# The attention outputs of a first token block: seven heads loaded during the last head, the eighth after it; the norm vectors loaded on another queue

## The chip, the cores and the metric

The kernel runs on one core of a Trainium2 chip. The metric is the device time of one execution in microseconds (us), lower is better. Besides TensorE (PE, with PEld for its weight loads), the core has VectorE (DVE), ScalarE (ACT), GpSimd (POOL) and SyncE (SP); nearly all transfers are issued by SP.

## What is computed

A network of two layers on a sequence of 1024 tokens with width 1024, in float32. Only the first layer's token mixer and what follows it matter here:

```python
def block(args):                       # 8 heads, blocks of 128 queries
    logits = einsum(q_nope, k_nope) + einsum(q_rope, k_rope)
    logits = where(chunk_mask, logits * scale, NEG_BIG)
    p = softmax(logits)
    return einsum('bhqk,bkhd->bqhd', p, v)
o = from_blocks(map(block)).reshape(b, s, 8 * 128)
mix = o @ w_o
h = layernorm(ALPHA * h + mix, ln_mix_g, ln_mix_b)
h = layernorm(ALPHA * h + swiglu(h), ln_ffn_g, ln_ffn_b)
```

## The kernel before

**Products.** Each matrix product is made of three matmuls: every operand x is split into a high part (ACT casts it) and a low part (DVE or POOL subtracts the high part from x), and high·high, high·low and low·high are added up in PSUM (`mm3`, lines 168 to 170).

**First attention.** `attention` (line 278) goes over the heads; each has eight blocks of 128 queries. For a block, `score_a` makes the scores and the softmax, `turn_a` the transposed, split probabilities (the casts and subtractions of lines 264 and 265), and after every second block `mix_a` makes the product with the values for a group of 256 queries. Its result goes through a tile `ob` with two buffers (the reduction of line 1319 on DVE) and is stored to `o_dr[0][group][head]` in DRAM (line 1320). The last head takes its blocks in the order 6, 7, 4, 5, 2, 3, 0, 1, so that group 3 is stored first, group 0 last. `fill` holds other work that is called after a given block.

**Output projection.** `out_proj` (line 298) follows. It loads the two vectors of the layer norm on the GpSimd queue (line 177), loads and splits `w_o` head by head (lines 142, 146 and 147; the splits of heads 6 and 7 are held behind the attention's last casts), and takes the eight token blocks in the same order. For a block it loads the outputs of all eight heads, 128 partitions by 8 by 128 values, into a tile `of` (line 319), splits them in two halves of four heads each into `oh` and `ol` (lines 323 and 324), loads the residual rows into `z` (line 330), makes two halves of 512 columns with 24 matmuls each, adds them to `z` (line 338) and normalises (`layer_norm`). The first block's splits are held behind the attention's last cast and last subtraction:

```python
                    if prev is None:
                        behind(i.ins, newest["hi"])
                        behind(j.ins, newest["lo"])
```

`behind` keeps program order and waits for nothing. The program is written in a framework that makes the waits itself and that orders the instructions of each engine by priority (the order of the calls) and by its own estimate of when an instruction can start; an engine then takes them in that order. Memory is given out in pools, and a tile waits for the last readers of what lay in its place.

**After it.** `ffn` takes the normalised blocks, first transposed by `raw_x`.

Of the kernel before, what the change touches and what calls it, by code (L numbers as in the profile page):

```python
# [9 lines left out]
F32 = mybir.dt.float32  # L10
# [6 lines left out]
P = 128  # L17
S = 1024
D = 1024
NTB = S // P  # L20
KD = D // P
H = 8
# [16 lines left out]
LAST_ORDER = (6, 7, 4, 5, 2, 3, 0, 1)  # L39
# [3 lines left out]
def trunk(  # L43
# [32 lines left out]
    nc = tc.nc  # L76
# [9 lines left out]
    late = edge.tile([P, 504], F32, tag="edge", name="edge")  # L86
# [21 lines left out]
    def f32(t):  # L108
        return t.bitcast(F32)

    def big_tile(name, dt=F32R):
        return big.tile([P, 2, 1024], dt, tag="big", name=name)
# [20 lines left out]
    def small(name, n=1):  # L133
        return sp.tile([P, 2], F32, tag="small", name=name, bufs=22)[:, :n]
# [40 lines left out]
    def bcast_row(pool, src, n, name, tag, eng=None):  # L175
        t = pool.tile([P, n], F32, tag=tag, name=name, bufs=1)
        (eng or nc.gpsimd).dma_start(t, src.partition_broadcast(P))
        return t

    def behind(i, j):  # L180

        tc.add_manual_dep(
            i, j.name,
            mybir.DependencyInfo(mybir.DependencyClass.NoSync, mybir.DependencyReason.DATA),
            reason="kept in program order",
        )
# [91 lines left out]
    def attention(score, turn, mix, fill, la, hp):  # L278


        blocks = [(h, i) for h in range(H - 1) for i in range(NTB)] + [(H - 1, i) for i in LAST_ORDER]
        for fn in fill.get(-1, ()):
            fn()
        for b in range(la):
            score(*blocks[b])
        for b, (h, i) in enumerate(blocks):
            if b and i % 2 == 0:
                mix(blocks[b - 1][0], blocks[b - 1][1] // 2)
            if b + la < len(blocks):
                with tc.high_priority(hp[0]):  # L290
                    score(*blocks[b + la])
            with tc.high_priority(hp[1]):
                turn(h, i)
            for fn in fill.get(b, ()):
                fn()
        mix(blocks[-1][0], blocks[-1][1] // 2)

    def out_proj(side, w_o, o_dram, x_src, x_dst, lng, lnb, xo):


        with tc.tile_pool(name="op0", bufs=2, side=side, reuse_waits="tile") as pool:
            g = bcast_row(pool, lng, D, "mg0", "g")
            b = bcast_row(pool, lnb, D, "mb0", "b")
            wo = []
            for h in range(H):
                dst = ()
                if h in (0, 1, 2, 3, 7):
                    t = big_tile(f"wo0_{h}")
                    dst = (t[:, 0], t[:, 1])
                elif h == 6:  # L310
                    t = pool.tile([P, 2, D], F32R, tag=f"wo{h}", name=f"wo0_{h}", bufs=1)
                    dst = (t[:, 0], t[:, 1])
                wo.append(load_w(w_o[h], 1024, f"wo0_{h}", *dst, after=("hi", "scale") if h > 5 else ()))
            prev = None
            for tb in LAST_ORDER:
                nm = f"a0_{tb}"
                of = pool.tile([P, H, P], F32, tag="of", name=f"of_{nm}", bufs=2)
                src = o_dram[tb // 2][:, :, (tb % 2) * P:(tb % 2) * P + P]
                loaded = nc.sync.dma_start(of, src.rearrange("h p q -> p h q")).ins
                ot = pool.tile([P, 2, D], F32R, tag="oh", name=f"oh_{nm}").rearrange("p a (h q) -> p a h q", h=H)  # L320
                oh, ol = ot[:, 0], ot[:, 1]
                for hs in (slice(0, 4), slice(4, 8)):
                    i = A.copy(oh[:, hs], of[:, hs])
                    j = V.tensor_tensor(ol[:, hs], of[:, hs], f32(oh[:, hs]), ALU.subtract)
                    if prev is None:
                        behind(i.ins, newest["hi"])
                        behind(j.ins, newest["lo"])
                zy = pool.tile([P, 2, D], F32, tag="zy", name=f"zy_{nm}")
                z, y = zy[:, 0], zy[:, 1]
                behind(nc.sync.dma_start(z, x_src[tb * P:(tb + 1) * P, :]).ins, loaded)  # L330
                sums = small(f"sum_{nm}", 2)
                junk = []
                for nh in range(2):
                    c = slice(nh * 512, nh * 512 + 512)
                    m = (ps_m if nh == 0 else ps_t)(f"zp_{nm}_{nh}")
                    junk.append(m)
                    mm3(m, [(oh[:, h, :], ol[:, h, :], wo[h][0][:, c], wo[h][1][:, c]) for h in range(H)])
                    V.scalar_tensor_tensor(
                        z[:, c], z[:, c], ALPHA, m, ALU.mult, ALU.add, accum_out=sums[:, nh:nh + 1]
                    )  # L340
                if tb == LAST_ORDER[-1]:
                    y = big_tile(f"y_{nm}", F32)[:, 0]
                layer_norm(z, sums, junk, y, g, b, nm, x_dst[tb * P:(tb + 1) * P, :])
                if prev is not None:
                    raw_x(prev[1], xo, prev[0], f"a0_{prev[0]}")
                prev = (tb, y)
        return lambda: raw_x(prev[1], xo, prev[0], f"a0_{prev[0]}")
# [733 lines left out]
    o_dr = [[dr.tile([H, P, 256], F32, name=f"o_dr{l}_{g}") for g in range(4)] for l in range(2)]  # L1081
    zero_dr = dr.tile([P, 512], F32, name="zero_dr")
    wo_dr = [dr.tile([P, 2, D], F32, name=f"wo_dr{h}") for h in range(H)]
    xs_dr = [dr.tile([S, D], F32, name=f"xs_dr{l}") for l in range(3)]


    lat4 = [[big_tile(f"c{p}{hf}").rearrange("p a (b t) -> p (a b) t", b=2) for hf in range(2)] for p in range(2)]
    ast = ExitStack()
    krp = ast.enter_context(tc.tile_pool(name="krp", bufs=1))
    lat2 = [big_tile("ck_hi"), krp.tile([P, 2, S], F32R, tag="cklo", name="ck_lo")]  # L1090
# [9 lines left out]
    with tc.tile_pool(name="a0", bufs=2, side="right") as pool:  # L1100
# [53 lines left out]
            return ms  # L1154

        def latents(tb, hq, hk):
            junk = pool.tile([P, 384], F32, tag="junk", name=f"junk{tb}")
            ssq = small(f"ssq{tb}", 2)
            A.activation(junk, hq[:, :384], AF.Square, accum_out=ssq[:, 0:1])
            A.activation(junk[:, :256], hk[:, :256], AF.Square, accum_out=ssq[:, 1:2])  # L1160
            ve = small(f"cve{tb}", 2)
            V.tensor_scalar(ve[:, 0:1], ssq[:, 0:1], 1.0 / RQ, RMS_EPS, ALU.mult, ALU.add)
            V.tensor_scalar(ve[:, 1:2], ssq[:, 1:2], 1.0 / RKV, RMS_EPS, ALU.mult, ALU.add)
            rs = small(f"crs{tb}", 2)
            G.tensor_tensor(rs, ve, mhalf, ALU.pow)
            cn = pool.tile([P, 768], F32, tag="cn", name=f"cn{tb}")
            ra = pool.tile([P, 64], F32, tag="ra", name=f"ra{tb}")
            rb = pool.tile([P, 64], F32, tag="rb", name=f"rb{tb}")
            V.tensor_tensor(ra, hk[:, 256:320], kt[:, tb, 0:64], ALU.mult)
            V.tensor_tensor(rb[:, 0:32], hk[:, 288:320], kt[:, tb, 64:96], ALU.mult)  # L1170
            V.tensor_tensor(rb[:, 32:64], hk[:, 256:288], kt[:, tb, 96:128], ALU.mult)
            V.tensor_tensor(cn[:, 640:704], ra, rb, ALU.add)
            V.tensor_tensor(cn[:, 704:768], ra, rb, ALU.add)
            V.scalar_tensor_tensor(cn[:, :384], hq[:, :384], rs[:, 0:1], gq, ALU.mult, ALU.mult)
            V.scalar_tensor_tensor(cn[:, 384:640], hk[:, :256], rs[:, 1:2], gk, ALU.mult, ALU.mult)
            return cn
# [46 lines left out]
    with ast as st:  # L1223
        pool = st.enter_context(tc.tile_pool(name="a1", bufs=2, reuse_waits="tile"))
# [99 lines left out]
        def at(slot, fn, *args):  # L1324
            fill.setdefault(slot, []).append(lambda: fn(*args))
# [9 lines left out]
        for h in range(1, H):  # L1335
            b = 8 * (h - 1)
# [17 lines left out]
            nc.sync.dma_start(zero_dr, f32(t[:, :512]))  # L1354

        at(14, store_zeros)
        attention(score_a, turn_a, mix_a, fill, 2, (0, 0))

    banks("ps2", PS_BUFS)
# [14 lines left out]
        return new_xT(pool, "f0")  # L1374

    xo, stacks = x_pools("m0", "right")
    pending = out_proj("left", w_o_a, o_dr[0], x, xs_dr[0], ln_mix_g[0], ln_mix_b[0], xo)
    xT, rest, normed = ffn("left", xo, stacks, pending, 0, xs_dr[0], xs_dr[1], ln_ffn_g[0], ln_ffn_b[0], next_x)


    banks("ps3", PS_BUFS_B)
    with ExitStack() as st:
        lp = st.enter_context(tc.tile_pool(name="b1l", bufs=5, reuse_waits="tile"))
        pool = st.enter_context(tc.tile_pool(name="b1", bufs=2, reuse_waits="tile"))
# [9 lines left out]
        for ql in q_lo:  # L1394
            for mp in range(2):
                b = slice(64 - mp * 64, 128 - mp * 64)
# [135 lines left out]
        for h in range(1, H):  # L1532
            b = 8 * (h - 1)
# [13 lines left out]
        first, second = LAST_ORDER[:2]  # L1547
# [6 lines left out]
        b = 8 * (H - 1) - 2  # L1554
# [11 lines left out]
    xo, stacks = x_pools("m1", "left")  # L1566
    pending = proj[0].rest(ln_mix_g[1], ln_mix_b[1], xo)
# [91 lines left out]
```

## Time and profile before

| | |
|---|---|
| median of 3 runs | 2265.44 us (2265.01 to 2267.45) |
| profiled execution, span from first to last instruction | 2269.7 us |
| PE busy | 2238.7 us, 99% of the span |
| DVE, ACT, POOL busy | 1593.1, 1007.1, 886.3 us |
| data moved | 289.25 MB |

The profiled execution's own time is given by its span alone; it lies 4.3 us over the median of the timed runs. Matmuls are pipelined, so a busy PE need not be one at its peak. A row of a timeline gives the start, the duration, the engine, the line, the operation, the tiles, and in brackets how long the engine had been idle and which instruction ended that.

### The profile page before, as it was taken

To read this page: it belongs to the slowest core of one execution; us is meant where nothing else is said; L and a number is where in the kernel's file an instruction comes from. 1 tells how busy PE (TensorE), PEld (TensorE's weight loads), DVE (VectorE), ACT (ScalarE), POOL (GpSimd) and SP (SyncE) were. 2 spreads that over 40 slices of the span, in tenths; PEclk is the share of its full clock that TensorE was granted. 3 is DMA by queue.
4 is the path that set the end of the run, shared out by engine and by line. 5 is a ranking of instruction groups with operands and counts; after the bars stand their busy time and mean duration, and the time that the engine had idled before them with its cause. 6 is when DMAs were issued, how large, how long until landed. Compare 5 with 4: busy or idle time off the path is not lost.

```text
span 2269.7 us, 30075 instructions
## 1 busy us (share of the span) xinstructions
PE 2238.7 (99%) x10850; PEld 1883.5 (83%) x10850; DVE 1593.1 (70%) x2944; ACT 1007.1 (44%) x2077; POOL 886.3 (39%) x711
## 2 busy tenths in 40 slices
PE   9999999999999999999999999999999999999998
PEld 9888897878888888887888888877778888888886
DVE  6677774596656667778578777676586666568778
ACT  4455563352333334445466656555442332334444
POOL 2243451104544445555333435321014444446552
PEclk9999999999999999999999999999999999999999
DMA  6121335334324138454311212153334323247544
GB/s 207 41 95 59 121 98 186 116 145 148 139 70 139 70 114 335 177 199 153 112 43 33 61 35 64 42 209 114 137 132 150 108 83 126 82 150 269 204 171 159
DMA packets 104420, 289.25 MB, mean 127 GB/s; under 512 B 8656, under 2 KB 32080, under 8 KB 93776
## 3 DMA queue, kind: packets, MB, share of 16 engines
q1 hardware_dynamic: 100272, 277.90, 35.0%
q0 software_dynamic: 4000, 9.44, 1.5%
q8 instruction: 85, 1.39, 0.2%
q14 instruction: 63, 0.52, 0.1%
HBM read 205.78 MB, written 77.33 MB: 125 GB/s over the span
## 4 chain that ended last, share of the span: by engine, by line
PE 46%; DVE 5%; issue 1%; DMA 1%; ACT 1%; POOL 1%; POOLq 0%; DVEq 0%; SPq 0%; ACTq 0%
PE gb L565 8%; PE gc L565 5%; PE dw L871 4%; PE ga L565 4%; PE zp_a L440 3%; PE dx L871 3%; PE s_b L239 3%; PE bp L168 2%; PE bp L170 2%; PE bp L169 2%; PE bv L1409 2%; PE dv L871 1%; PE dy L871 1%; PE o_b L274 1%; PE pt_b L173 1%
## 5 line engine op out<-in xcount | busy, mean ns | idle before, releaser
L521 ACT CAST op_g<-gr 128x512 fp32r<-128x512 f32 x240 | 147.5, 622 | 403.5 <-PE gb L565 225.4
L521 POOL TENSOR_TENSOR op_g<-gr,op_g 128x512 fp32r<-128x512 f32 x104 | 146.1, 1410 | 303.4 <-DVE tmp L661 160.0
L521 DVE TENSOR_TENSOR op_h<-rh,op_h 128x512 fp32r<-128x512 f32 x154 | 164.0, 1090 | 58.8 <-ACT op_h L521 58.7
L565 PE MATMUL ga<-xh_m,op_g 128*128 128x512 f32 x512 | 168.0, 389 | 0.0
L871 PE MATMUL dw<-op_w_t,op_h 128*128 128x512 f32 x660 | 153.1, 391 | 1.8 <-DVE op_h L521 1.8
L521 ACT CAST op_h<-rh 128x512 fp32r<-128x512 f32 x154 | 92.3, 619 | 139.9 <-DMA rh<-h_dr 42.8
L871 PEld LDWEIGHTS dw<-op_w_t,op_h 128*128 128x128 f32 x660 | 123.2, 188 | 28.3 <-DVE op_h L521 2.8
L245 ACT ACTIVATE l_b<-l_b,mx_b 128x256 f32<-128x256 f32 (+7 forms) x128 | 99.5, 777 | 73.5 <-DVE mx_b L242 70.4
L521 POOL TENSOR_TENSOR op_w_t<-tt,op_w_t 128x512 fp32r<-128x512 f32 x66 | 98.2, 1490 | 81.2 <-ACT op_w_t L521 81.2
L565 PE MATMUL gb<-t3h_f,op_g 128*128 128x512 f32 x352 | 117.0, 394 | 3.6 <-ACT tmp L675 2.9
L1462 POOL TENSOR_SCALAR l_b<-l_b,r_b,cst 128x128 f32<-128x128 f32 (+3 forms) x64 | 52.5, 821 | 174.2 <-DVE r_b L247 152.9
L871 PE MATMUL dx<-op_w_b,op_h 128*128 128x512 f32 x528 | 120.3, 389 | 0.0
L565 PE MATMUL gb<-t4h_f,op_g 128*128 128x512 f32 x352 | 115.7, 390 | 0.8 <-DVE tmp L652 0.8
L871 PEld LDWEIGHTS dx<-op_w_b,op_h 128*128 128x128 f32 x528 | 99.1, 188 | 20.6
L521 DVE TENSOR_TENSOR op_g<-gr,op_g 128x512 fp32r<-128x512 f32 x136 | 110.3, 811 | 8.4 <-ACT op_g L521 8.1
L565 PE MATMUL gc<-b22h_f,op_g 128*128 128x512 f32 x352 | 115.5, 389 | 0.0
L565 PE MATMUL gc<-t1h_f,op_g 128*128 128x512 f32 x352 | 115.5, 389 | 0.0
L565 PE MATMUL gb<-t2h_f,op_g 128*128 128x512 f32 x352 | 115.1, 389 | 0.0
L521 POOL TENSOR_TENSOR op_g<-s,op_g 128x512 fp32r<-128x512 f32 x40 | 54.3, 1358 | 151.8 <-ACT op_g L521 151.7
L565 PEld LDWEIGHTS ga<-xh_m,op_g 128*128 128x128 f32 x512 | 96.1, 188 | 19.9
L168 PE MATMUL bp<-xT_f,h_wb 128*128 128x512 f32 x256 | 103.2, 403 | 0.2
L169 PE MATMUL bp<-xT_f,h_wb 128*128 128x512 f32 x256 | 101.9, 398 | 0.0
(389 smaller groups left out, 6567.9 us busy)
## 6 DMA issues: line engine op xcount, KB each, us to landing
gr<-in_w_gu SPq DMA_DIRECT2D x44, 1024.0 KB, 6.9
rh<-h_dr SPq DMA_DIRECT2D x28, 1024.0 KB, 5.0
h_dr<-sh SPq DMA_DIRECT2D x22, 1024.0 KB, 4.9
h_dr<-hp SPq DMA_DIRECT2D x22, 768.0 KB, 4.0
tt<-in_w_dn SPq DMA_DIRECT2D x22, 512.0 KB, 8.2
rh<-h_dr SPq DMA_DIRECT2D x14, 768.0 KB, 4.4
z<-xs_dr SPq DMA_DIRECT2D x16, 512.0 KB, 11.3
rw_b<-in_w_dn SPq DMA_DIRECT2D x8, 1024.0 KB, 8.1
```

The costliest lines, as they stand in the source:

```text
L168: T.matmul(ps_out, lh, rh, start=(i == 0), stop=False)
L169: T.matmul(ps_out, lh, rl, start=False, stop=False)
L170: T.matmul(ps_out, ll, rh, start=False, stop=(i == n - 1))
L173: T.transpose(ps_out, in_, ident)
L239: T.matmul(s[:, :w], lh, rh[:, ks], start=(j == 0), stop=(j == len(q_pass) - 1))
L245: newest["exp"] = A.activation(l[:, :n], l[:, :n], AF.Exp, bias=mx, scale=-1.0, accum_out=sm).ins
L440: T.matmul(m, a[:, h, :], self.wo[h][w][:, c], start=(start and h == heads[0] and a is oh and w == 0), stop=(stop and h == heads[-1] and a ...
L521: return A.copy(hi, src).ins, eng.tensor_tensor(lo, src, f32(hi), ALU.subtract).ins
L565: T.matmul(o, w[:, a, kc], x[b][:, k, :], start=(first and k == 0 and (a, b) == (0, 0)), stop=(k == 3 and a == 1), skip_group_check=True,)
L871: i = T.matmul(o, h[:, a, c], w[:, b_], start=(first and (a, b_) == (0, 0)), stop=(last and a == 1), skip_group_check=True,).ins
L1409: T.matmul(m, xT[0][hf][:, k, c], w[k], start=(k == 0), stop=False, skip_group_check=True)
L1462: G.tensor_scalar(l1[:, :n], l1[:, :n], r1, nlam, ALU.mult, ALU.mult)
```

## The change

Of the first block's outputs (block 6 of group 3), the heads 0 to 6 are loaded by a call in the `fill` of block 57 of the attention, which is the last head's second block, into a tile in a pool of its own that is opened ahead of the attention. `out_proj` gets this tile and loads only head 7 into it; the other seven blocks go through `of` as before. The two norm vectors are no longer loaded on the GpSimd queue at the start of `out_proj`, but by SP, kept behind the first block's load of `z`. A scratch tile of an earlier stage (`junk`) moves into a tile that exists already (`late`), and the pools that stand on the new one lie 4 KB per partition higher.

```diff
-    def out_proj(side, w_o, o_dram, x_src, x_dst, lng, lnb, xo):
+    def of_load(of, o_dram, tb, h0=0, h1=H):
+
+        src = o_dram[tb // 2][h0:h1, :, (tb % 2) * P:(tb % 2) * P + P]
+        return nc.sync.dma_start(of[:, h0:h1], src.rearrange("h p q -> p h q")).ins
+
+    def out_proj(side, w_o, o_dram, x_src, x_dst, lng, lnb, xo, first):
...
-            g = bcast_row(pool, lng, D, "mg0", "g")
-            b = bcast_row(pool, lnb, D, "mb0", "b")
+            g, b = (pool.tile([P, D], F32, tag=t, name=f"m{t}0", bufs=1) for t in "gb")
...
-                of = pool.tile([P, H, P], F32, tag="of", name=f"of_{nm}", bufs=2)
-                src = o_dram[tb // 2][:, :, (tb % 2) * P:(tb % 2) * P + P]
-                loaded = nc.sync.dma_start(of, src.rearrange("h p q -> p h q")).ins
+                of, h0 = first, H - 1
+                if prev is not None:
+                    of, h0 = pool.tile([P, H, P], F32, tag="of", name=f"of_{nm}", bufs=2), 0
+                before = of_load(of, o_dram, tb, h0)
...
-                behind(nc.sync.dma_start(z, x_src[tb * P:(tb + 1) * P, :]).ins, loaded)
+                loaded = nc.sync.dma_start(z, x_src[tb * P:(tb + 1) * P, :]).ins
+                behind(loaded, before)
+                if prev is None:
+                    for t, v in ((g, lng), (b, lnb)):
+                        behind(nc.sync.dma_start(t, v.partition_broadcast(P)).ins, loaded)
...
+    fst = ExitStack()
+    firstp = fst.enter_context(tc.tile_pool(name="of0", bufs=1, reuse_waits="tile"))
...
-            junk = pool.tile([P, 384], F32, tag="junk", name=f"junk{tb}")
+            junk = late[:, :384]
...
+        first_of = firstp.tile([P, H, P], F32, tag="of", name="of_first")
+        at(8 * H - 7, of_load, first_of, o_dr[0], LAST_ORDER[0], 0, H - 1)
         attention(score_a, turn_a, mix_a, fill, 2, (0, 0))
...
-    pending = out_proj("left", w_o_a, o_dr[0], x, xs_dr[0], ln_mix_g[0], ln_mix_b[0], xo)
+    pending = out_proj("left", w_o_a, o_dr[0], x, xs_dr[0], ln_mix_g[0], ln_mix_b[0], xo,
+                       first_of)
+    fst.close()
```

## Rows read from the trace of the kernel before

**Rows 1.** The page: busy time; then PE's waits, with total, times, longest.

```profile
PE 2238.7 (99%) x10850; PEld 1883.5 (83%) x10850; DVE 1593.1 (70%) x2944; ACT 1007.1 (44%) x2077; POOL 886.3 (39%) x711
...
PE zp_a L168 <- ACT oh_a L323: 4.2, 1, 4.2
```

**Rows 2.** Timeline of PE, ACT and POOL from the attention's end on.

```profile
345.49 0.37 ACT L264 CAST pt_a<-pt_a 128x256 fp32r<-128x256 f32 x1 [0.61 <-PE pt_a L173]
345.76 1.99 ACT L146 CAST wo<-r_wo 128x1024 fp32r<-128x1024 f32 x2
346.89 4.64 POOL L147 TENSOR_TENSOR wo<-r_wo,wo 128x1024 fp32r<-128x1024 f32 x2 [3.19 <-ACT wo L146]
346.95 0.23 PE L275 MATMUL o_a<-pt_a,vl 128*128 128x128 f32 x1
350.72 1.14 ACT L323 CAST oh_a<-of_a 128x512 fp32r<-128x512 f32 x2 [2.97 <-DMA of_a<-o_dr]
351.39 0.80 PE L168 MATMUL zp_a<-wo,oh_a 128*128 128x512 f32 x1 [4.21 <-ACT oh_a L323]
352.41 0.63 PE L170 MATMUL zp_a<-wo,oh_a 128*128 128x512 f32 x1
355.40 0.40 PE L168 MATMUL zp_a<-wo,oh_a 128*128 128x512 f32 x1
359.50 0.39 PE L168 MATMUL zp_a<-wo,oh_a 128*128 128x512 f32 x1
```

**Rows 3.** Timeline of DVE over the same stretch.

```profile
346.35 0.69 DVE L1319 TENSOR_REDUCE ob<-o_a 128x256 f32<-128x512 f32 x1
351.37 1.32 DVE L324 TENSOR_TENSOR oh_a<-of_a,oh_a 128x512 fp32r<-128x512 f32 x2 [4.33 <-ACT oh_a L323]
...
355.31 0.68 DVE L1319 TENSOR_REDUCE ob<-o_a 128x256 f32<-128x512 f32 x1
```

**Rows 4.** Timeline of SP's queue; start and time to the end of the last issue.

```profile
332.50 8.77 SPq L1320 DMA_DIRECT2D o_dr<-ob  x2
342.69 0.37 SPq L319 DMA_DIRECT2D of_a<-o_dr  x1
343.11 0.58 SPq L330 DMA_DIRECT2D zy_a<-in_x  x1
343.74 0.67 SPq L319 DMA_DIRECT2D of_a<-o_dr  x1
344.45 2.33 SPq L330 DMA_DIRECT2D zy_a<-in_x  x1
346.88 2.98 SPq L1320 DMA_DIRECT2D o_dr<-ob  x2
```

**Rows 5.** DMA issues from 296 to 362: KB each, median us to landing.

```profile
o_dr<-ob SPq DMA_DIRECT2D x9, 128.0 KB, 1.7
zy_a<-in_x SPq DMA_DIRECT2D x2, 512.0 KB, 9.5
mg<-in_ln_mix_g POOLq DMA_DIRECT2D x1, 512.0 KB, 4.5
mb<-in_ln_mix_b POOLq DMA_DIRECT2D x1, 512.0 KB, 7.3
```

**Rows 6.** Line 319, all eight loads: us to landing.

```profile
DMA to landing us min/median/max: 3.8/4.6/9.7
```

**Rows 7.** Stretches: busy us of PE, PEld, DVE, ACT, POOL, granted clock, DMA share, GB/s.

```profile
335.00:340.00 5.00, 5.00 (x33) 4.45 (x32) 3.56 (x14) 3.37 (x10) 1.65 (x3) 1.00 0.01 3
...
348.00:349.00 1.00, 0.00 (x0) 0.00 (x0) 0.00 (x0) 0.00 (x0) 1.00 (x1) 0.78 0.91 265
...
355.00:356.00 1.00, 1.00 (x5) 0.81 (x4) 0.99 (x2) 0.00 (x0) 0.00 (x0) 0.80 0.97 398
...
1070.00:1071.00 1.00, 0.61 (x3) 0.52 (x4) 1.00 (x3) 0.00 (x0) 0.00 (x0) 1.00 0.00 0
```

**Rows 8.** Timeline of PE: a second idle stretch, far from the change.

```profile
1070.39 11.20 PE L871 MATMUL dw<-op_w_t,op_h 128*128 128x512 f32 x48 [1.50 <-DVE op_h L521]
```

## The prediction

> **What bounds the kernel now.** The page comes first: PE is busy 99% of the span, so a change helps only where it shortens PE's idle time or its time at the lower clock. PE's own waits, sorted by length, come next: the longest single one, 4.2 us, is of the output projection's first matmul for ACT's cast of line 323 [rows 1]. I then read the timeline around it. The attention's last matmul ends at 346.95 + 0.23 = 347.18, the projection's first starts at 351.39, and that is the 4.21 of its bracket. ACT itself is through with the splits of `w_o` at 345.76 + 1.99 = 347.75 and then waits for a transfer, the load of `of`, until 350.72 [rows 2]. SP's queue says why: this load is issued at 342.69, after head 7's store of group 3, whose issue ends at 332.50 + 8.77 = 341.27 [rows 4]; it lands some 8.0 us later, where the fastest of the eight loads of this line took 3.8 [rows 6]. It shares its time with the two norm vectors and with the next three loads of 512 KB [rows 4, 5].
>
> [...]
>
> **The change, part by part.**
>
> *The seven heads' load.* Its last source is head 6's store of group 3, issued at 332.50 [rows 4]; a store lands in 1.7 [rows 5], so SP can issue the load from about 334.2. SP has nothing else to issue until 340.95 or so, and the DMA engines are 1% busy from 335 to 340 [rows 4, 7]. 448 KB take between 3.8 and 9.7, the fastest and the slowest load of the line [rows 6]; I take 3.8, as the engines are free: landed at 338.0, at worst at 343.9. Either is ahead of 347.75, when ACT could use it, so this load costs nothing. SP's wait for the store holds up only the store at 341.
>
> *Head 7's load.* It is issued where the whole load was, 342.69. For 64 KB there is no row; the nearest are the 128 KB store (1.7) and the whole load in its crowd (8.0): landed between 344.4 and 350.7. I take 344.4, since now nothing of the crowd is in front of it. Only heads 4 to 7 need it, from the thirteenth matmul on.
>
> *The splits.* ACT still ends the `w_o` casts at 347.75; these come earlier in the order of the calls and are held behind the same cast, so I leave them in front. In the trace PE starts 0.67 after ACT's first cast does (350.72 to 351.39) [rows 2]. So PE starts at 347.75 + 0.67 = **348.42**, and its idle time shrinks from 4.21 to 1.24.
>
> *The clock.* The nearest idle stretch is one of 1.50 us that ends at 1070.39 [rows 8], and the clock stays at 1.00 in it and behind it [rows 7]. I take it that 1.24 leaves the clock up, too. [...]
>
> *DVE.* The third matmul needs the first low part. DVE's two subtractions take 1.32, 0.66 each [rows 3]. In the trace the third matmul starts 0.38 behind the first one's end (351.37 + 0.66 = 352.03, 352.41) [rows 2, 3]; some of that is the slow clock's, and I take 0.2. From 348.40 this gives 349.26, against 348.42 + 0.46 = 348.88 for an unhindered one: a stall of 0.38, a new wait that the late ACT had partly covered. The second half is split by 349.8, and the thirteenth matmul is due at 351.5.
>
> *Norm vectors and the second block.* POOL loses two DMA issues, at a time when it is not what PE waits for: nothing. On SP the vectors add 1 MB in front of the second block's loads, but 448 KB less are in front of them in all, and the 1 MB was in the same crowd before. The second block's `of` was issued at 343.74 and could land 9.7 later, at 353.4 [rows 4, 6]. PE comes to it 48 matmuls after its start, at about 359.7, and splitting takes 1.3: five microseconds are left. The first block's `z` (343.11 + 9.5 = 352.6 at the old pace) is needed after 24 matmuls, at 354.3 [rows 4, 5]. The scratch tile and the higher pools: nothing, as ACT alone writes the scratch, in order, and the loads and splits start after the attention's last scores.
>
> **The sum.** The tenth matmul starts at 348.42 + 2.05 + 0.38 = 350.85 instead of 355.40: **4.55 us** earlier, made of 2.97 of idle time and 1.96 of clock less 0.38. Everything behind it follows PE: the projection, the norms, the ffn's operands. The profiled execution of 2269.7 would have 2265.1, the median of 2265.44 **2260.9**, 0.20% less. That is right at the 0.2% (4.5 us) which a measurement of this kernel can tell from no change.
>
> **The rivals.**
>
> 1. *ACT takes the block's casts ahead of the `w_o` splits.* They could start at 345.86, after the last cast of line 264 [rows 2]. PE would go on at 347.2 with almost no gap; DVE's reduction until 347.04 [rows 3] and POOL's split of head 7, which ends 1.1 later than 351.53 [rows 2], would cost some 0.5 together. Gain 6.2 − 0.5 = 5.7, **2259.7**. Against it: the order of the calls.
>
> 2. *The change doesn't do what it says*: the first cast waits for head 7's load too, and this one lands as late as the whole load did, at 350.7. Then nothing is gained, **2265.4**. For it: SP's issues follow each other within a microsecond, and all share the DMA engines. Against it: it is the first of them in the queue.
>
> 3. *The clock falls in spite of the short gap.* Then only the idle time is won, 2.97 or so, **2262.5**.
>
> 4. *The other side: DVE takes the last group's reduction (line 1319) ahead of the low parts.* It needs the buffer of `ob` that group 2's store reads, issued at 346.88 behind SP's loads [rows 4]. Before, it ran at 355.31, after all four subtractions [rows 3]. In front of them it would hold PE's third matmul until the store has landed, plus 0.69 + 0.66 + 0.2. At 1.7 for the landing that is 350.1, still a gain of 3.6; at the 9.7 of the slowest load in the crowd it is 358.1, and with seven more steps at the slow clock, 0.43 each, the tenth starts at 361.1: 5.7 lost, **2271.1**. It turns into a loss where the store lands after about 350.8. [...]
>
> 5. *Stages far behind come in another order*, since the framework orders by estimated times, which move. Either sign, **2256 to 2270**; nothing in the profile speaks for a side.
>
> **How the numbers follow.** My forecast has 0.54; as it lies on the bound, I count 0.28 of it as faster by over 0.2% and 0.26 as within. Rival 1 has 0.14 (faster), rival 2 0.06 (within), rival 3 0.13 (within), rival 4 0.06 (half within, half slower), rival 5 0.07 (0.03 faster, 0.04 slower). Faster 0.28 + 0.14 + 0.03 = 0.45, within 0.26 + 0.06 + 0.13 + 0.03 = 0.48, slower 0.07. The predicted time is the likeliest case's, 2260.9. The range holds the forecast, rival 1 and rival 3 with about 1 us beside each for the stalls that I could only bound, 2258.6 to 2263.6; what it leaves out are rivals 2, 4 and 5, under 0.2.
>
> **What would show it.** In the profile after: the seven heads' load issued near 334 and landed before 344; ACT's casts of line 323 right behind line 146 at 347.8; PE idle for about 1.2 us before its first matmul of line 168, the clock at 1.00 throughout, ten matmuls within 2.5 us; PE without a gap at the second block. A cast of line 323 ahead of line 146 is rival 1, a clock at the lower level rival 3, a reduction of line 1319 ahead of line 324 rival 4. The prediction is wrong if PE's gap stays above 3 us, or if the gap closes and the span does not follow, because a later wait has grown by as much.

## The result: 0.14% slower, and what the profile after shows

The changed kernel takes 2269.47 us (median of 21 runs, 2265.76 to 2271.86), the kernel before 2266.28 in runs beside it (21 runs, 2263.12 to 2267.96). The ratio is 1.0014 with a 95% interval of 1.0008 to 1.0019: some 3.2 us slower, where 4.5 us faster was forecast. The spans of the two profiled executions (2266.2 and 2269.7) stand the other way round; this is a matter of these executions, as a second one of each shows below, so I compare stretches and not spans.

Page, then PE's waits, of the changed kernel (total, times, longest). They answer to [rows 1]:

```profile
PE 2236.2 (99%) x10850; PEld 1880.9 (83%) x10850; DVE 1591.6 (70%) x2944; ACT 1008.2 (44%) x2077; POOL 887.0 (39%) x709
...
PE v L168 <- DVE qrb L1254: 4.2, 1, 4.2
...
PE zp_a L170 <- DVE oh_a L329: 0.8, 1, 0.8
PE zp_a L168 <- ACT oh_a L328: 0.7, 1, 0.7
```

The 4.2 us at the output projection are gone, as forecast; 0.7 and 0.8 are left of them. But a wait of the same length has come up in another place: that of PE's first matmul for the values `v`, 270 us earlier.

Timeline of the changed kernel at the handover: PE, ACT, DVE, POOL, SP's queue. It answers to [rows 2 to 4]:

```profile
350.23 0.22 PE L275 MATMUL o_a<-pt_a,vl 128*128 128x128 f32 x1
351.20 0.50 PE L168 MATMUL zp_a<-wo,oh_a 128*128 128x512 f32 x1 [0.74 <-ACT oh_a L328]
352.75 0.50 PE L170 MATMUL zp_a<-wo,oh_a 128*128 128x512 f32 x1 [0.82 <-DVE oh_a L329]
355.46 0.63 PE L168 MATMUL zp_a<-wo,oh_a 128*128 128x512 f32 x1
...
348.63 2.00 ACT L146 CAST wo<-r_wo 128x1024 fp32r<-128x1024 f32 x2
350.53 1.14 ACT L328 CAST oh_a<-of_first 128x512 fp32r<-128x512 f32 x2
...
351.18 4.30 DVE L329 TENSOR_TENSOR oh_a<-of_first,oh_a 128x512 fp32r<-128x512 f32 x2 [0.57 <-ACT oh_a L328]
356.64 0.69 DVE L1330 TENSOR_REDUCE ob<-o_a 128x256 f32<-128x512 f32 x1 [1.16 <-DMA o_dr<-ob]
...
349.76 5.16 POOL L147 TENSOR_TENSOR wo<-r_wo,wo 128x1024 fp32r<-128x1024 f32 x2 [2.11 <-ACT wo L146]
...
337.96 0.38 SPq L301 DMA_DIRECT2D of_first<-o_dr  x1
346.21 0.32 SPq L301 DMA_DIRECT2D of_first<-o_dr  x1
```

The seven heads are loaded 12.5 us before the attention ends (350.23 + 0.22 = 350.45), and ACT's casts of line 328 follow line 146 without a wait for a transfer. The projection's tenth matmul starts at 355.46, 5.01 behind the attention's end; before it was 8.22 [rows 2]. So the handover gained 3.2 us. Two things are worse than forecast: the two subtractions of line 329 take 4.30 together, beside POOL's, where they took 1.32 [rows 3], and the clock falls (below).

The same kernel's timeline around the new wait: SP's queue, ACT's last square, DVE, PE (`edge` is the name of the tile `late` in the rows):

```profile
20.77 0.33 SPq L1221 DMA_DIRECT2D cst<-in_g_sub  x1
23.11 6.91 SPq L1124 DMA_DIRECT2D x<-in_xt  x3
...
73.60 0.39 ACT L1171 ACTIVATE edge<-hk 128x256 f32<-128x256 f32 x1
...
74.10 0.33 SPq L1223 DMA_DIRECT2D edge<-in_lam_q  x1
...
75.42 0.43 SPq L1223 DMA_DIRECT2D edge<-in_lam_k  x1
...
77.50 0.23 DVE L1228 TENSOR_TENSOR edge<-edge 128x64 f32<-128x64 f32 x1 [0.67 <-DMA edge<-in_lam_k]
79.57 0.23 DVE L1228 TENSOR_TENSOR edge<-edge 128x64 f32<-128x64 f32 x1 [1.85 <-DMA edge<-in_lam_k]
...
80.59 0.68 DVE L1252 TENSOR_TENSOR qra<-qr,cos 128x512 f32<-128x512 f32 x1
81.28 2.79 DVE L1254 TENSOR_TENSOR qrb<-qr,sin 32x512 f32<-32x512 f32 x4
...
84.12 0.58 PE L168 MATMUL v<-h_wa,c 128*128 128x256 f32 x1 [4.25 <-DVE qrb L1254]
```

SP's longest wait in the changed kernel up to 125 us (what waited, for what: total, times, longest):

```profile
SPq L1223 <- ACT edge L1171: 36.3, 1, 36.3
```

The same in the kernel before, the first and the last of the four loads, and `v`:

```profile
21.93 0.33 SPq L1212 DMA_DIRECT2D edge<-in_lam_q  x1
...
25.68 0.33 SPq L1212 DMA_DIRECT2D edge<-in_lam_k  x1
...
81.20 0.39 PE L168 MATMUL v<-h_wa,c 128*128 128x256 f32 x1 [0.34 <-DVE qrb L1243]
```

Line 1223 loads four small vectors (for a factor called lambda, wanted in the second layer only) into the tile `late`. In the kernel before, these loads are issued from 21.93 to 25.68. Now `late` is also the scratch into which ACT writes the squares of `latents` (72.98 to 73.99 for the last block, lines 1170 and 1171), so SP issues the loads only at 74.10. Their products on DVE (line 1228) stand in front of the rope (lines 1252 and 1254), wait there for the transfers, and PE's `v` waits for the rope.

Stretches of the changed kernel (busy us of PE, PEld, DVE, ACT, POOL, granted clock, DMA share, GB/s):

```profile
83.00:84.00 1.00, 0.00 (x0) 0.00 (x0) 0.99 (x2) 0.00 (x0) 0.00 (x0) 0.82 0.00 0
84.00:85.00 1.00, 0.88 (x4) 0.88 (x5) 0.97 (x3) 0.00 (x0) 0.76 (x1) 0.50 0.00 0
...
353.00:354.00 1.00, 1.00 (x4) 0.81 (x4) 1.00 (x1) 0.00 (x0) 1.00 (x1) 0.65 0.86 234
354.00:355.00 1.00, 1.00 (x3) 0.76 (x3) 1.00 (x1) 0.00 (x0) 0.93 (x1) 0.50 1.12 344
```

The clock falls to its lower level (0.50) at both places; before, it fell at the second alone [rows 7] and was 1.00 in every stretch from 76 to 89.

### The profile page after: what moved, and what is told of

Same layout as the page of the kernel before. It is cut to its first block, busy times and chain, and to the rows that moved or that the text cites. A ratio compares the mean times of both kernels' runs of the same rounds, so it can differ in the third digit from the quotient of the medians.

```text
span 2266.2 us, 30088 instructions
## 1 busy us (share of the span) xinstructions
PE 2236.2 (99%) x10850; PEld 1880.9 (83%) x10850; DVE 1591.6 (70%) x2944; ACT 1008.2 (44%) x2077; POOL 887.0 (39%) x709
## 4 chain that ended last, share of the span: by engine, by line
PE 86%; DVE 7%; DMA 2%; issue 2%; ACT 2%; POOL 0%; SPq 0%; POOLq 0%; DVEq 0%; ACTq 0%
PE gb L574 15%; PE gc L574 11%; PE ga L574 10%; PE dw L880 7%; PE zp_a L449 3%; PE s_a L239 3%; PE dv L880 3%; PE dx L880 3%; PE s_b L239 2%; PE bp L168 2%; PE bp L170 2%; PE bp L169 2%; PE bv L1424 2%; PE o_a L274 1%; PE dy L880 1%
```

## The experiments

No kernel leaves out a part of the computation. The theory after the two traces: the loss is the scratch's move alone, and the handover's part of the change gains about what was forecast. The rivals: the move costs nothing and the projection's later parts eat the gain, or the load of seven heads isn't what gains it.

**1. The scratch alone.** The kernel before with one line changed.

```diff
-            junk = pool.tile([P, 384], F32, tag="junk", name=f"junk{tb}")
+            junk = late[:, :384]
```

> The kernel before, with only the scratch of the squares moved into the tile that the lambda loads use; loads and norm vectors as before. Theory A (the moved scratch makes the lambda loads wait for the last square, and DVE, which has their arithmetic queued ahead of the rope, holds PE): PE waits some 4 us at 80 and the time is 4.3 us over before, about 2270.5 against 2266.3. Theory B (the scratch is harmless, the loss lies at the handover, in SP's longer queue): no such wait, 2266.3.

Measured: 2273.64 us beside 2267.25, ratio 1.0029 (1.0020 to 1.0039), some 6.6 us slower. PE's timeline in it has the wait of the changed kernel, and the handover's gap as before (3.9):

```profile
84.80 0.58 PE L168 MATMUL v<-h_wa,c 128*128 128x256 f32 x1 [4.81 <-DVE qrb L1243]
```

So the one line costs more than the whole change lost, and more than the 4.3 expected: 5.9 in stretch A of the table below, with the wait at 4.81 (0.34 before), and 1.0 in stretch C.

**2. The change with a scratch of its own.** The squares go into the block's own tile `cn`, which is written only afterwards.

```diff
-            junk = late[:, :384]
+            cn = pool.tile([P, 768], F32, tag="cn", name=f"cn{tb}")
+            junk = cn[:, :384]
...
-            cn = pool.tile([P, 768], F32, tag="cn", name=f"cn{tb}")
```

> The changed kernel, with the squares of a block written into the tile that later takes its normalised latents, instead of the lambda tile; all else as in the change. Theory A: the wait at 80 goes, 4.3 us come back, 2263 to 2265. Theory B: 2269.5 as with the change.

Measured: 2263.79 beside 2267.25, ratio 0.9979 (0.9970 to 0.9988). The loads of line 1223 are back at 22.60 to 26.29, and `v` waits 0.35. PE's timeline at the handover (the attention ends at 345.75):

```profile
346.47 0.50 PE L168 MATMUL zp_a<-wo,oh_a 128*128 128x512 f32 x1 [0.72 <-ACT oh_a L328]
...
348.01 0.50 PE L170 MATMUL zp_a<-wo,oh_a 128*128 128x512 f32 x1 [0.81 <-DVE oh_a L329]
```

The gaps are those of the changed kernel, but the clock stays at 1.00, and the tenth matmul starts at 349.73, 3.98 behind the attention's end: 4.24 gained of the 4.55 forecast.

**3. The products held back.** The change as it is, but the lambda products may not stand ahead of the attention's last subtraction; the loads stay late.

```diff
-            V.tensor_tensor(lv[2 * i], lv[2 * i], lv[2 * i + 1], ALU.mult)
+            j = V.tensor_tensor(lv[2 * i], lv[2 * i], lv[2 * i + 1], ALU.mult)
+            behind(j.ins, newest["lo"])
```

> The changed kernel with the scratch where the change puts it, but the two products of the lambda vectors kept behind the attention's low parts at the block where they are called. Theory A in its narrow form (it is DVE's order that costs, not the late loads): as the run with a scratch of its own, 2263 to 2265, though the lambda loads are still issued at 74. If the late loads themselves cost: 2268 to 2270.

Measured: 2265.51 beside 2267.25, ratio 0.9986 (0.9977 to 0.9995). `v` waits 0.41. The late loads as such cost nothing: it is the place of their products on DVE, in front of the rope, that makes them cost in stretch A.

**4. The block's casts ahead of the last `w_o` splits.** Experiment 2, and the splits of heads 6 and 7 called behind the first block's. This is the first rival of the prediction, made on purpose, and it takes POOL's subtraction away from beside DVE's.

```diff
-            for h in range(H):
+            def load_wo(h):
...
+            for h in range(6):
+                load_wo(h)
...
+                if prev is None:
+                    load_wo(6)
+                    load_wo(7)
```

> As the run with a scratch of its own, and the w_o splits of heads 6 and 7 called after the first block's splits, so that ACT casts the block first and POOL subtracts for w_o only after DVE is done with the block. Theory C (at the handover DVE's two subtractions run at 1.5 and 2.9 us instead of 0.7 because POOL subtracts beside them, and that wait takes the clock down): both at 0.7, PE's gap under 0.4 us in all, the clock at 1.00, 2260 to 2261. Rival D (they are slow because of the transfers or of the tile's place): still over 1.4 us, 2263 to 2265.

Measured: 2262.88 beside 2267.25, ratio 0.9976 (0.9966 to 0.9986). PE has no gap at the handover. Timeline of DVE and POOL:

```profile
345.13 1.28 DVE L333 TENSOR_TENSOR oh_a<-of_first,oh_a 128x512 fp32r<-128x512 f32 x2
...
346.45 4.75 POOL L147 TENSOR_TENSOR wo<-r_wo,wo 128x1024 fp32r<-128x1024 f32 x2 [3.15 <-ACT wo L146]
```

With POOL behind them, the two subtractions take 1.28 instead of 4.30. The time is above the 2260 to 2261 expected, and its interval overlaps that of experiment 2, so it is the trace that tells the theory from its rival, and not the time.

**5. The norm vectors alone.** The kernel before, the two vectors loaded by SP behind the first `z`; no load of seven heads, and its own scratch.

```diff
-            g = bcast_row(pool, lng, D, "mg0", "g")
-            b = bcast_row(pool, lnb, D, "mb0", "b")
+            g, b = (pool.tile([P, D], F32, tag=t, name=f"m{t}0", bufs=1) for t in "gb")
...
+                if prev is None:
+                    for t, v in ((g, lng), (b, lnb)):
+                        behind(nc.sync.dma_start(t, v.partition_broadcast(P)).ins, zl)
```

> The kernel before with the two norm vectors alone moved: they go to SP, behind the first block's z; there is no load of seven heads, and the latents' scratch is as before. Theory that the crowd made the whole load late: with the vectors' 1 MB gone from in front of it, the load of 512 KB, issued near 342.7, lands in the 3.8 to 4.6 us of the fastest and the median load of its line, so at 346.5 to 347.3 and ahead of ACT's last split of w_o at 347.75; then the gap of 4.21 shrinks to about 1.2 as with the seven heads' load, and the time is some 3 to 4 us under the kernel before. Rival, that the early load of seven heads is what wins: the whole load still lands after 349, the gap stays above 2.5 us, and the time is within 1.5 us of the kernel before.

Measured: 2260.99 beside 2266.54, ratio 0.9978 (0.9969 to 0.9987). Timeline of SP's queue, ACT and PE:

```profile
341.78 0.37 SPq L318 DMA_DIRECT2D of_a<-o_dr  x1
...
344.13 2.00 ACT L146 CAST wo<-r_wo 128x1024 fp32r<-128x1024 f32 x2
346.03 1.14 ACT L322 CAST oh_a<-of_a 128x512 fp32r<-128x512 f32 x2
...
346.70 0.50 PE L168 MATMUL zp_a<-wo,oh_a 128*128 128x512 f32 x1 [0.71 <-ACT oh_a L322]
```

DMA issues of this kernel from 341 to 343 (KB, us to landing):

```profile
of_a<-o_dr SPq DMA_DIRECT2D x1, 512.0 KB, 3.9
```

The whole load of eight heads lands 3.9 us from its issue (8.0 before), and ACT goes from the splits to the casts without a wait. With 1 MB of vectors out of its way, the load as it was is in time, and the early one isn't needed. The gap is 0.71 where 1.2 was expected, and the gain is larger than the 3 to 4 us expected.

**6 and 7. The vectors back on POOL's queue**, in experiment 2 (so that the seven heads stand alone) and in experiment 4. The edit is that of experiment 5 the other way round.

> The second kernel of the experiments (own scratch) with the norm vectors back on POOL at the head of the projection, so that of the change the load of seven heads stands alone. Theory that the early load wins: the first cast is free at 347.7 or so as with the vectors behind, the tenth matmul of the projection starts about 4 us after the attention's last, and the time is that of the kernel with its own scratch, 3 to 4 us under the kernel before. Rival, that head 7's load and the z of the first block are held up by the vectors' 1 MB: a wait of PE for the low part of heads 4 to 7 shows in the second half of the block, and 1 to 3 us of the gain are lost.

> The kernel with the casts first (own scratch, the last two w_o splits called behind the first block's), with the norm vectors back on POOL. If the vectors' place is worth nothing, it is within 1 us of that kernel, 4 to 5 us under the kernel before, with no gap of PE at the handover. If head 7's load is held up by the vectors, the casts of heads 4 to 7 stand in front of the w_o splits on ACT and wait there: PE then waits for the weights of heads 6 and 7 too, and 2 us or more are lost against it.

Measured: the seven heads alone 2264.91 beside 2266.54, ratio 0.9993 (0.9984 to 1.0002), not told from no change; with the casts first 2262.82, ratio 0.9987 (0.9978 to 0.9995). Both times miss the forecasts of the theories (3 to 4 us under the kernel before, and within 1 us of experiment 4) and lie where the rivals put them. Head 7's load of 64 KB now takes 4.1 and 3.8 to land (1.7 in the changed kernel), and PE's first gap in the former is 1.15. In the former no wait for heads 4 to 7 shows, so the rival's mechanism is not there. In the latter it is there in small: ACT's second cast waits 0.11 us for head 7's load, the `w_o` splits come later, and PE waits for the last of them, which it does for 0.06 and 0.07 in experiments 4 and 10:

```profile
352.64 0.50 PE L169 MATMUL zp_a<-wo,oh_a 128*128 128x512 f32 x1 [0.43 <-POOL wo L147]
```

Stretch B is 0.7 longer than in experiment 4 for it; the 2.0 to 2.5 us that the ratios show (with intervals that overlap) are not all accounted for. In these profiled executions, the seven heads alone gain 2.5 us at the handover (stretch B of the table below), as much as the vectors alone: each of the two edits closes most of the gap by itself.

**8 to 10. Experiments 2, 5 and 4 again, on one chip.**

> The changed kernel with its own scratch again, beside the vectors alone on the same chip and with a second profiled execution. Theory that the load of seven heads is worth nothing once the vectors are out of the way: within 1.5 us of the vectors alone, 3 to 5 us under the kernel before. Rival, that the load is worth the gap in which it lands: 2 us or more under the vectors alone. In the profile: the gaps of 0.7 and 0.8 us stay; if the clock falls behind them this time, the fall is a matter of the execution and not of the kernel; if it stays up again, something that differs between the kernels holds it.

> The kernel before with the two norm vectors alone moved, again, beside the own scratch on the same chip. By both theories 3 to 6 us under the kernel before. In the profile: the whole load landed before ACT is through with the w_o splits, gaps of 0.7 and 0.8 us; whether the clock falls as it did in this kernel's first profile shows if this belongs to the kernel or to the execution.

> The casts first, again, on the same chip as the own scratch. If the two gaps at the handover cost what the profiles show (0.7 + 0.8, and up to 1.4 more where the clock falls behind them), it is 1.5 to 3 us under the own scratch; if the executions that are timed mostly keep the clock and give the gaps back later, it is within 1 us of it.

Measured beside 2265.93: own scratch 2263.37, ratio 0.9987 (0.9979 to 0.9996); vectors alone 2261.33, ratio 0.9976 (0.9967 to 0.9985); casts first 2260.48, ratio 0.9978 (0.9968 to 0.9987). The own scratch is 2 us over the vectors alone, so beside the vectors the load of seven heads adds nothing that the time shows. The casts first are 2.0 us under the own scratch by the ratios, as expected. Both differences are between kernels whose intervals overlap. Stretches of the second executions, first own scratch, then vectors alone:

```profile
349.00:350.00 1.00, 1.00 (x6) 0.84 (x5) 1.00 (x1) 0.00 (x0) 0.60 (x1) 1.00 1.18 394
```

```profile
349.00:350.00 1.00, 1.00 (x3) 0.77 (x3) 1.00 (x1) 0.00 (x0) 0.46 (x1) 0.50 1.06 318
```

Both have gaps of 0.74 and 0.81; the clock fell in both executions of the vectors alone and in neither of the own scratch.

**11 and 12. The kernel before and the changed one, profiled again** (one run each).

> A second profiled execution of the kernel before. If the wait of 2.9 us at 1680 and the one of 1.5 us at 1070 belong to the kernel, they are there again, and the span is 2269 to 2270; if they are a matter of the execution, one or both are shorter or gone, and the span is 2 to 7 us shorter. The handover's gap of 4.2 us with the clock's fall behind it comes again by every theory.

> A second profiled execution of the changed kernel. The wait of 4.2 us for the rope at 84, the gaps of 0.7 and 0.8 us at the handover and the slow subtractions come again by the theory of the shared tile and of the engines side by side. If the clock's fall behind the handover belongs to the kernel, it is there again; if not, the tenth matmul comes about 1 us earlier. The waits at 1070 and 1680 are there or not, as the execution goes.

Measured: spans of 2261.9 and 2266.3, now in the order of the timed runs. The kernel before differs from its first execution by 7.8 us: the 1.50 at 1070 [rows 8] and a wait of 2.93 at 1682.77 are gone, and its gap at the handover is 3.96. The changed kernel waits 4.47 for the rope, and its clock stays up at the handover this time. PE's timeline, and a stretch, of that execution:

```profile
84.25 0.58 PE L168 MATMUL v<-h_wa,c 128*128 128x256 f32 x1 [4.47 <-DVE qrb L1254]
...
352.30 0.50 PE L168 MATMUL zp_a<-wo,oh_a 128*128 128x512 f32 x1 [0.73 <-ACT oh_a L328]
353.84 0.50 PE L170 MATMUL zp_a<-wo,oh_a 128*128 128x512 f32 x1 [0.81 <-DVE oh_a L329]
...
355.56 0.39 PE L168 MATMUL zp_a<-wo,oh_a 128*128 128x512 f32 x1
```

```profile
354.00:355.00 1.00, 1.00 (x5) 0.82 (x6) 1.00 (x1) 0.00 (x0) 1.00 (x1) 1.00 0.79 248
```

**All of them in three stretches.** From the starts of PE's matmuls: A from the last `hk` to the last `o_a` (the new wait lies in it), B on to the last `zp_a` of this projection, C from the first `dw` to the first `dv` in the ffn (some 30 us from 950 on). Two values are two executions; the sum is against the kernel before (means), beside the ratio times 2266.

| kernel | A | B | C | sum | measured |
|---|---|---|---|---|---|
| before | 273.24, 273.24 | 98.60, 98.61 | 30.55, 30.45 | | |
| changed | 277.50, 278.71 | 95.97, 94.42 | 31.87, 31.68 | +2.7 | +3.2 |
| 1 scratch alone | 279.15 | 99.55 | 31.50 | +7.9 | +6.6 |
| 2, 8 own scratch | 272.88, 272.86 | 94.43, 94.44 | 31.43, 31.45 | −3.6 | −4.8, −2.9 |
| 3 products held | 273.22 | 94.42 | 31.90 | −2.8 | −3.2 |
| 4, 10 casts first | 272.87, 272.89 | 92.69, 92.68 | 31.59, 31.71 | −5.1 | −5.4, −5.0 |
| 5, 9 vectors alone | 272.91, 272.90 | 95.94, 95.95 | 30.51, 30.43 | −3.0 | −5.0, −5.4 |
| 6 seven heads alone | 273.17 | 96.09 | 31.82 | −1.3 | −1.6 |
| 7 heads, casts first | 273.15 | 93.37 | 31.43 | −4.4 | −2.9 |

The three stretches give every kernel's time within 1.5 us but that of the vectors alone, which is some 2 us better than its sum. Its two profiled executions took 2264.52 and 2262.62, both above their medians, and had the clock down at the handover, at 1.5 us each (below); that most of the timed ones keep it up would account for the difference, but no trace shows those. What is not in them comes and goes from one execution of the same kernel to the next (the waits at 1070 and 1680), but for the second layer's attention, which is 0.3 to 1.3 longer in all these profiles than in the two of before.

Stretch C is a side effect of the scratch, too: one load of 768 KB, `rw_t`, takes longer to land in every kernel without the old scratch tile (7.1 to 7.6 us in ten executions) than with it (6.1 to 6.2 in four). DMA issues of that stretch, the kernel before and the changed one, second executions (KB, us to landing):

```profile
rw_t<-in_w_dn SPq DMA_DIRECT2D x1, 768.0 KB, 6.1
```

```profile
rw_t<-in_w_dn SPq DMA_DIRECT2D x1, 768.0 KB, 7.4
```

DVE's additions of line 841 wait for this load (idle for 1.55 in the kernel before and 2.79 in the changed one, in these executions), and PE's matmul of `dw` waits for DVE: 0.23 to 0.30 before and 1.47 to 1.66 in the changed kernel. It gives 0.9 to 1.4 of loss, also where the scratch has another place (experiments 2 to 4). Why the load takes longer isn't known; that the tiles lie elsewhere with the scratch gone is only a guess, and it wasn't tried.

## Why the prediction was wrong

**The step that failed** is "The scratch tile and the higher pools: nothing, as ACT alone writes the scratch, in order, and the loads and splits start after the attention's last scores." I asked who writes the scratch, and not who else writes the tile that it moved into. `late` is filled by four loads on SP, whose products stand on DVE's queue ahead of the rope. Cost: 4.3 to 5.5 us in stretch A, wait and slow clock together (the granted clock is at 0.50 from 84 to 87 in the first execution and from 83 to 89 in the second), and 1.2 to 1.4 in stretch C. Experiments 1 to 3 show the part in A: the line alone brings it, another scratch takes it away, and so does moving the products while the loads stay late. The part in C comes with the old scratch tile's going, wherever the scratch is put (experiments 1 to 3); why is open. No rival had it; the loss on record (the reduction ahead of the low parts) was another mechanism.

**The seven heads' load and head 7's**: right. Issued 12.5 us before the attention's end (13.0 forecast), landed in 3.7 (3.8 forecast), ahead of ACT; head 7 landed in 1.7.

**The splits**: right in order, with a gap of 0.74 where 1.24 was forecast, as ACT ends the `w_o` splits 0.2 behind the attention (350.63 and 350.45) where it was 0.6 [rows 2]. This goes with the vectors: the gap is 0.71 to 0.74 in the executions with them on SP's queue and the `w_o` splits first, and 1.15 with them on POOL's (experiment 6), near the forecast.

**DVE's stall**: right in place, mis-sized, 0.82 for 0.38. I took the 0.66 of one subtraction from a stretch in which POOL had all but ended, and costed POOL beside it at nothing. Even there the first of the two took 0.72 (the longest of line 324's sixteen, which have a median of 0.68) and ended at 351.37 + 0.72 = 352.09, 0.56 behind POOL's 351.53 [rows 2, 3]; read one by one, the two would have shown it. The two lines' own views in the changed kernel (ns min/median/max, first and last start), DVE's for the first block and the other seven, POOL's for `wo`:

```profile
L329 DVE TENSOR_TENSOR oh_a<-of_a,oh_a x14: 679/682/693, 357.2 to 425.1; 128x512 fp32r<-128x512 f32 x14
...
L329 DVE TENSOR_TENSOR oh_a<-of_first,oh_a x2: 1519/2189/2859, 351.2 to 352.6; 128x512 fp32r<-128x512 f32 x2
...
L147 POOL TENSOR_TENSOR wo<-r_wo,wo x6: 2383/2404/2837, 311.2 to 352.1; 128x1024 fp32r<-128x1024 f32 x6
```

They end in turn. POOL's first ends at 349.76 + 2.38 = 352.14, DVE's first at 351.18 + 1.52 = 352.70; POOL's second, 0.43 longer than usual, ends at 349.76 + 5.16 = 354.92, DVE's second at 351.18 + 4.30 = 355.48, each of DVE's 0.56 behind POOL's. The 0.56 comes again within 0.02 in all eight executions that have the two side by side, and the mean of DVE's two is 2.18 to 2.19 in each of them. What makes the one end behind the other, no run shows. The prediction should have priced the first low part by the 0.56 of the kernel before, at 0.56 behind the end of POOL's first. Experiment 4 takes POOL away from there: 1.28 for both, and no stall.

**The clock**: that these gaps leave it up held in the changed kernel's second execution and in experiments 2, 3 and 8; it fell in the first one and in 5, 6 and 9, at 1.5 us each in stretch B (95.97 against 94.42). So the third rival has, in the changed kernel, one execution of two. The changed kernel's gaps were 0.74 and 0.82 in the execution in which the clock fell to 0.50, and 0.73 and 0.81 in the one in which it stayed at 1.00, so the 1.50 us at 1070 [rows 7, 8] were no proof that a gap of this length leaves it up. Why the own scratch kept the clock twice and the vectors alone lost it twice stays open.

**The sum at the handover**: 4.55 forecast; 3.2 and 4.2 in the changed kernel's two executions, 4.24 in experiment 2. This part was right, up to the clock; that it came so near has some luck in it, as the shorter gap (0.5) and the longer stall (0.44) make up for each other. Its 2.05, and the 0.46 in the stall's 0.38, are nine and two steps of 0.228 us, which is what eighteen steps of the kernel before take from 355.40 to 359.50 (4.10 in all); its 1.96 is what the first nine steps there, 4.01 from 351.39 to 355.40, take beyond that [rows 2], with a granted clock of 0.50 from 351 to 355, 1.00 from 355.4 on, and one wait for DVE. With the idle 4.21 this makes the 6.2 of the first rival.

**The norm vectors**, costed at nothing, are mis-sized: alone they gain as much at the handover as the seven heads alone (2.66 and 2.51 in stretch B), and 5 us in the time, where the seven heads alone are not told from no change. My reading that the load "shares its time with the two norm vectors" had the cause; I then let the early load carry all of the gain and did not ask what the other edit gives by itself. At the handover the two are two ways to one gain, and it can be had once.

**The rivals.** The first one's order did not come by itself; made by hand it gains 1.75 us more in stretch B (1.15 forecast), of which the timed runs show 0.6 and 2.1, with intervals that overlap both times. The second, that nothing is gained, did not happen. The fourth: DVE's reduction did wait for its store (idle 1.16 at 356.64; the store issued at 348.73 took 7.8 to land), but behind the first block's low parts, where PE had work. The fifth, another order far behind: I found none that costs PE; stretch C is later data in the same order.

Of the signs that I named, the early load, the casts right behind line 146 and the second block without a gap came true, and PE's gap was shorter. The clock did not stay at 1.00 in the first execution, and ten matmuls within 2.5 us came in neither: the tenth starts 4.26 and 3.26 behind the first, with the stall in it. "If the gap closes and the span does not follow, because a later wait has grown by as much" is what happened, except that the wait is an earlier one.

## What to carry to other kernels

Before a tile is shared, list all who write and read it, transfers above all, and look at what stands behind their users on each engine's queue: memory that is given back cheaply is paid for with order. When a change has several parts, price each as if it stood alone: here two were ways to the same gain at the handover, and the one that looked like tidying up held the loss. The version to keep is the smallest, the two vectors behind `z`, 0.22% and 0.24% under the kernel before in two measurements.

## What the runs showed of the hardware

DVE's two subtractions took 4.3 us beside POOL's, in all eight executions, of five kernels, that had the two side by side, and 1.28 with POOL's behind them. Behind a gap of 0.71 to 0.74 us and one of 0.81 or 0.82, with 0.7 us of matmuls between, the clock fell in three executions (to 0.50 in the changed kernel's first) and stayed up in four (at 1.00 in its second). A load of 768 KB took 7.1 to 7.6 us to land, and 6.1 to 6.2 in kernels that differ in a scratch tile some 880 us earlier. Two executions of the kernel before differed by 7.8 us in their spans, 4.4 of it in waits of 1.5 and 2.9 us that came and went with nothing changed.
